# Two pairs of a feed-forward layer as eight block products, and the order of loads and splits at the turn to its down projection

## The chip, the cores and the metric

One core of a Trainium2 chip runs the whole program. The metric is the device time of one execution in microseconds (us). Engines are named PE (TensorE, matrix products), DVE (VectorE), ACT (ScalarE), POOL (GpSimd) and SP (SyncE, which issues the DMAs).

## The reference, cut to what matters

The program is one step of a two-layer decoder over 1024 prompt tokens and 8 x 4 sample tokens, 1056 in all, in float32 with a model width of 1024 and an inner width of 2816. Each layer has a mixer, a feed-forward block with a convolution over three tokens, and a gate. The change lies in the feed-forward block:

```python
def conv_ffn(xn, prefix, w_up, conv_w, conv_b, w_down):
    u = xn @ w_up                                   # (tokens, 5632)
    ext = jnp.concatenate([prefix, u], axis=1)
    c = conv_b + ext[:, 0:L] * conv_w[0]
    for k in range(1, CONV_W):
        c = c + ext[:, k:k + L] * conv_w[k]
    gate, val = jnp.split(c, 2, axis=-1)
    return (jax.nn.gelu(gate) * val) @ w_down, ext[:, -CONV_BUF:]
```

## The kernel before, in words

**Products.** Tokens lie in the free dimension, channels in the partitions, in tiles of 128. A float32 product is made of three products of rounded parts: high x high, low x high and high x low; for that every operand is split, the high part by a copy on ACT, the low part by a subtraction on DVE (`parts_of`, L585 and L586, in the up projection; `split`, L145 and L146, for the down weights).

**The up projection.** `ffn` walks over 22 pairs, each a gate tile and the value tile that belongs to it. A pair is a 2 x 2 block product: the 1024 channels in two halves of four tiles, the tokens in two halves N1 and N2 of 528 (H). `prod` (L666) is one block product over four channel tiles, 4 x 3 parts x 2 chunks of 264 columns = 24 matmuls (L672). `plain`, which pair 0 uses, takes eight such products, 192 matmuls. `unit`, used by pairs 1 to 21, takes seven, 168 matmuls, in the manner of Strassen and Winograd; for that it needs sums of weight blocks (`sums`, L603 to L606, on POOL, new for each pair) and sums of token blocks T1 to T4 (`token_sums`, L618, with DVE lines L640 to L643, splits at L647 and L648; `first_sums`, L655), formed once per layer from the normalized tokens. T1 overwrites the N2 half of the first four channel tiles of `xh` and `xl`, so it can be written only when `plain` has read them; T2 and T3 go into tiles `tk`, T4 into `t4h` and `t4l`. In `token_sums` the raw sums use the scratch of the convolution (`cg`, `ext`, `t4`). Results X, Y, Z and `aux` leave PSUM into `ext` (L699 on DVE in layer 0, L697 on ACT in layer 1), and the convolution runs on them: one step on ACT (L709), two on DVE (L711), for the gate `cg` and the value `cv`, then gelu (L716) and the product (L721), whose result `act_out` stores in DRAM as `ad`. Layer 0 scales by the norm factor R after the products, layer 1 before them (`normed`).

**The turn.** The last unit calls `end()`, which is `turn` (L828): `act_in` loads the activations of inner tiles 0 and 1 back (`ar`) and splits them into `ah` and `al`; `down_block` loads and splits a block of the down weights (`wr` into `wh` and `wl`); the residuals `hd` are loaded back into `h` by eight DMAs. Then `down` (L885) forms `mm` (L162) and adds it to `h` (L907), with 36 matmuls for the first two tiles of `h`.

**Order.** Each engine runs its instructions in program order. That order is made by a scheduler which simulates a timeline and places each instruction where its time comes up; `tc.issue_after` forces one instruction behind another. `late` is a list of instructions behind which the first splits are held.

## Time and profile before

| | us |
|---|---|
| median of 3 runs (2258.25 to 2262.13) | 2260.67 |
| the profiled execution | 2264.66 |
| its span | 2262.8 |
| PE busy in the span | 2170.3 (96%) |
| DVE busy | 1709.6 (76%) |
| ACT busy | 994.3 (44%) |
| POOL busy | 723.1 (32%) |

The profiled execution is 4 us above the median; what lies outside its span is 1.9 us. Times within the span, such as 133.10, are counted from its start. The granted clock of PE is given as a share of 2.4 GHz.

### The profile page before, as it was taken

How to read it: one execution, taken by the hardware profiler on the slowest of the kernel's cores; microseconds unless marked ns; L12 is line 12 of the kernel's file. 1: busy time of each engine (PE TensorE's matmuls, PEld its weight loads, DVE VectorE, ACT ScalarE, POOL GpSimd, SP SyncE). 2: the span in 40 equal slices, each digit the busy share in tenths (PEclk: the TensorE clock that was granted, in tenths of full speed). 3: DMA queues.
4: the chain of work that ended last, by engine and by line, in shares of the span. 5: the costliest groups of instructions: out<-in, count | busy, mean ns of one | idle time of the engine just before them, and what ended most of it. 6: DMA issues, size and time to landing. Idle time of an engine off the chain costs nothing.

```text
span 2262.8 us, 38188 instructions
## 1 busy us (share of the span) xinstructions
PE 2170.3 (96%) x15141; PEld 2112.4 (93%) x15141; DVE 1709.6 (76%) x2435; ACT 994.3 (44%) x1815; POOL 723.1 (32%) x752
## 2 busy tenths in 40 slices
PE   8979999999999999999989998899999999999999
PEld 7879999999899999999977898899999999999898
DVE  5889999999756677567689629788888876666843
ACT  6543343434321235346689625545454542121532
POOL 1435555554000013313467432544443420000400
PEclk7889999999999999999999999899999999999999
DMA  4322222222662311322111342122222227222121
GB/s 143 112 57 67 77 86 77 76 77 77 226 213 86 105 57 62 100 62 42 38 40 36 116 122 72 48 86 72 81 77 86 77 104 217 90 90 82 57 84 40
DMA packets 220006, 198.95 MB, mean 88 GB/s; under 512 B 38899, under 2 KB 190276, under 8 KB 219659
## 3 DMA queue, kind: packets, MB, share of 16 engines
q1 hardware_dynamic: 219827, 196.51, 27.9%
q8 instruction: 119, 1.95, 0.4%
q14 instruction: 60, 0.49, 0.1%
HBM read 150.42 MB, written 51.59 MB: 89 GB/s over the span
## 4 chain that ended last, share of the span: by engine, by line
PE 78%; DVE 14%; ACT 4%; issue 2%; POOL 1%; DMA 1%; SPq 0%; ACTq 0%; DVEq 0%; POOLq 0%
PE mm L162 22%; PE x L672 11%; PE y L672 10%; PE z L672 10%; PE aux L672 5%; PE ub L168 3%; PE ub L170 3%; PE ub L169 3%; DVE xl L225 2%; PE dps L359 2%; PE qkp L168 1%; PE qkp L170 1%; PE qkp L169 1%; DVE h L917 1%; DVE wl L146 1%
## 5 line engine op out<-in xcount | busy, mean ns | idle before, releaser
L907 DVE TENSOR_TENSOR h<-mm,h 128x1056 f32<-128x1056 f32 x160 | 200.6, 1256 | 159.7 <-PE mm L162 159.7
L242 POOL TENSOR_TENSOR acc<-acc,sq 128x352 f32<-128x352 f32 x84 | 92.0, 1099 | 640.0 <-ACT sq L241 638.6
L162 PE MATMUL mm<-ah,wh 128*128 128x352 f32 x960 | 209.8, 328 | 11.8 <-ACT ah L585 10.1
L162 PE MATMUL mm<-al,wh 128*128 128x352 f32 x960 | 208.6, 325 | 0.0
L162 PE MATMUL mm<-ah,wl 128*128 128x352 f32 x960 | 206.8, 324 | 0.0
L711 DVE SCALAR_TENSOR_TENSOR cg<-ext,cw,cg 128x1072 f32<-128x1072 f32 x88 | 181.7, 2065 | 4.7 <-ACT cg L709 4.6
L145 ACT ACTIVATE wh<-wr 128x1024 fp32r<-128x1024 f32 x77 | 81.1, 1055 | 236.2 <-PE mm L162 203.9
L162 PEld LDWEIGHTS mm<-ah,wh 128*128 128x128 f32 x960 | 164.1, 190 | 14.1 <-ACT ah L585 10.5
L692 POOL COPY sto<-ext 128x2 f32<-128x2 f32 x88 | 57.0, 648 | 338.4 <-ACT ext L697 202.7
L162 PEld LDWEIGHTS mm<-al,wh 128*128 128x128 f32 x960 | 164.6, 190 | 0.4 <-DVE al L586 0.4
L162 PEld LDWEIGHTS mm<-ah,wl 128*128 128x128 f32 x960 | 163.7, 189 | 0.0
L672 PE MATMUL x<-xl,wh 128*128 128x264 f32 x704 | 146.2, 289 | 3.6 <-DVE xl L1626 3.6
L672 PE MATMUL x<-xh,wh 128*128 128x264 f32 x704 | 146.2, 290 | 2.7 <-ACT p L749 1.3
L672 PE MATMUL x<-xh,wl 128*128 128x264 f32 x704 | 145.7, 288 | 0.0
L168 PE MATMUL ub<-xh,wh 128*128 128x352 f32 x432 | 142.1, 329 | 0.1
L170 PE MATMUL ub<-xh,wl 128*128 128x352 f32 x432 | 140.5, 325 | 0.0
L169 PE MATMUL ub<-xl,wh 128*128 128x352 f32 x432 | 139.4, 323 | 0.0
L691 POOL COPY ext<-sin 128x16 f32<-128x16 f32 x88 | 81.2, 922 | 139.2 <-DVE cg L711 61.3
L711 DVE SCALAR_TENSOR_TENSOR cv<-ext,cw,cv 128x1072 f32<-128x1072 f32 x88 | 120.6, 1370 | 3.7 <-ACT cv L709 3.1
L585 ACT ACTIVATE ah<-ar 128x1024 fp32r<-128x1024 f32 x88 | 51.8, 636 | 160.6 <-PE mm L162 141.1
L672 PEld LDWEIGHTS x<-xl,wh 128*128 128x128 f32 x704 | 112.0, 192 | 4.2 <-DVE xl L1626 4.1
L672 PEld LDWEIGHTS x<-xh,wh 128*128 128x128 f32 x704 | 111.5, 193 | 3.7 <-ACT p L749 1.6
(391 smaller groups left out, 6578.6 us busy)
## 6 DMA issues: line engine op xcount, KB each, us to landing
ad<-cv SPq DMA_DIRECT2D x44, 536.0 KB
ar<-ad SPq DMA_DIRECT2D x44, 536.0 KB
wr<-in_w_up_dram SPq DMA_DIRECT2D x46, 512.0 KB
wr<-in_w_down_dram SPq DMA_DIRECT2D x44, 512.0 KB
vr<-in_w_up_dram SPq DMA_DIRECT2D x42, 512.0 KB
h<-hd SPq DMA_DIRECT2D x24, 528.0 KB
wr<-in_w_ple_gate_dram SPq DMA_DIRECT2D x16, 512.0 KB
hd<-h SPq DMA_DIRECT2D x13, 528.0 KB
```

Of the source, the lines that this page charges most:

```text
L145: A.activation(out=wh, in_=flat, func=AF.Copy)
L162: PE.matmul(ps[:, c, :C], w[k], b[k][:, c * C:(c + 1) * C], start=st, stop=sp)
L168: PE.matmul(ps, wh[k], bh[k][:, cs], start=k == 0, stop=False)
L169: PE.matmul(ps, wh[k], bl[k][:, cs], start=False, stop=False)
L170: PE.matmul(ps, wl[k], bh[k][:, cs], start=False, stop=k == nk - 1)
L242: G.tensor_tensor(out=st["acc"][:, cs], in0=st["acc"][:, cs], in1=sq, op=ALU.add)
L585: A.activation(out=h_, in_=src, func=AF.Copy)
L672: PE.matmul(ps[c], x[:, k0 + k, :], y[k][:, c * HC:(c + 1) * HC], start=first and n == 0, stop=n == 11, skip_group_check=True)
L691: G.tensor_copy(out=es[:, :, 0:2], in_=sin[:, j, :].rearrange("p (s r) -> p s r", r=2))
L692: G.tensor_copy(out=sto[:, j, 0:2], in_=e[:, NP:NP + 2])
L711: V.scalar_tensor_tensor(out=c, in0=e[:, k:k + CO], scalar=cw[:, k, j:j + 1], in1=c, op0=ALU.mult, op1=ALU.add)
L907: V.tensor_tensor(out=three(hm_(f, m)), in0=ps[:, :, :C], in1=three(hm_(f, m)), op=ALU.add)
```

## The change

Pair 1 becomes a second `plain`, so that units run from pair 2 on, all in one order of products; the special order that unit 1 had (L785 to L799) is gone. `token_sums` is called twice, for channel tiles 0 and 1 within pair 0 and 2 and 3 within pair 1, with scratch of its own, `tt`, which has one buffer; `first_sums` follows pair 1's products. At the turn the first weight block's DMA is issued behind the second activation load, the last gate convolution and the last `act_out` behind the second activation's split on ACT, and the residual loads, as before, behind that load.

```diff
@@ -615,16 +618,12 @@
-        def token_sums():
-
-            t1s = []
-            for k in range(4):
+        def token_sums(ks):
+
+            for k in ks:
                 K = k + 4
-                if k % 2:
-                    t2, t3, t4 = exts[0][:, 2:2 + H], exts[0][:, 2 + H:2 + T], exts[1][:, 2:2 + H]
-                else:
-                    c = long("cg", CO)
-                    t2, t3, t4 = c[:, :H], c[:, H:T], long("t4", H)
+                tt = long("tt", 3 * H)
+                t2, t3, t4 = [tt[:, n * H:(n + 1) * H] for n in range(3)]
...
@@ -727,8 +725,7 @@
-            t1s = token_sums()
-            first_sums(t1s)
+            token_sums(range(2 * i, 2 * i + 2))
             times(two(eg[:, 2:2 + H]), x_ps, two(R1))
@@ -737,6 +734,8 @@
             cg = gate_conv(i)
             times(two(ev[:, 2:2 + H]), z_ps, two(R1))
+            if i:
+                first_sums()
             act_out(i, cg)
@@ -760,46 +759,29 @@
-            if i > 1:
-                prod(Y, wc, 4, T2, True)
...
-            else:
-
-                prod(Z, wb, 4, B22, True)
-                A.activation(out=two(p5), in_=z_ps, func=AF.Copy)
...
-            cg = gate_conv(i)
+            prod(W, wv, 0, T4, True)
+            es = ExitStack()
             if not more:
-                end()
+                es.enter_context(tc.issue_after(end().ins))
+            with es:
+                cg = gate_conv(i)
@@ -807,7 +789,10 @@
             if more:
                 wv_ = val_parts(raws.pop(0))
-            act_out(i, cg)
+                act_out(i, cg)
+            else:
+                with tc.issue_after(pre[1].ins):
+                    act_out(i, cg)
@@ -833,17 +819,17 @@
             act_in(0)
-            came = act_in(1)
-            pre.append(down_block(0, 0))
+            came, split_ = act_in(1)
+            pre.extend([down_block(0, 0, came), split_])
             pairs(f)
             with tc.issue_after(came.ins):
                 for m in range(DT):
                     dma(hm_(f, m), hd[m])
+            return split_
@@ -856,12 +842,15 @@
-        S = sums(w1)
         plain(0, wg, wv)
         late.clear()
-        w = (big_parts(w1[0]), s12_parts(S), big_parts(S[:, 1024:2048]), val_parts(w1))
-        raws = [load(2)]
-        for i in range(1, FT):
+        w2 = load(2)
+        wg, wv = big_parts(w1[0]), big_parts(w1[1])
+        S = sums(w2)
+        plain(1, wg, wv)
+        w = (big_parts(w2[0]), s12_parts(S), big_parts(S[:, 1024:2048]), val_parts(w2))
+        raws = [load(3)]
+        for i in range(2, FT):
             w = unit(i, *w, raws, turn)
@@ -886,7 +875,7 @@
-                return pre.pop() if pre else down_block(g, half)
+                return pre.pop(0) if g + half == 0 else down_block(g, half)
```

Three places of the order. In the rows of the changed kernel line numbers are its own: L670 is L672 of before, L697 is L699, L709 is L711, L707 is L709, L714 is L716, L719 is L721, L588 and L589 are L585 and L586, L804 and L805 are the halves of the activations' split, L860 is L871, L896 is L907, L789 is L807 and L787 is L805.

PE where pair 0 ends in layer 0, before; `vh` and `vl` are the split value weights of pair 1:

```order
L672 MATMUL z<-xh,wh 128x264 x2
L672 MATMUL z<-xl,wh 128x264 x2
L672 MATMUL z<-xh,wl 128x264 x2
L672 MATMUL aux<-t4h,vh 128x264 x2
L672 MATMUL aux<-t4l,vh 128x264 x2
L672 MATMUL aux<-t4h,vl 128x264 x2
```

Z is pair 0's last product; `aux` is the first of pair 1's.

The same place now:

```order
L670 MATMUL z<-xh,wh 128x264 x2
L670 MATMUL z<-xl,wh 128x264 x2
L670 MATMUL z<-xh,wl 128x264 x2
L670 MATMUL x<-xh,wh 128x264 x2
L670 MATMUL x<-xl,wh 128x264 x2
L670 MATMUL x<-xh,wl 128x264 x2
```

What follows pair 0's Z was the product with T4; now it is pair 1's X with the plain tokens.

DVE beside it in layer 0, before: token sums and their splits, in a row:

```order
L641 SCALAR_TENSOR_TENSOR cg<-h,gains,u_1423 128x528
L642 SCALAR_TENSOR_TENSOR cg<-h,gains,cv 128x528
L648 TENSOR_TENSOR t4l<-ext_1152,t4h 128x528
L641 SCALAR_TENSOR_TENSOR ext_1151<-h,gains,vv 128x528
L642 SCALAR_TENSOR_TENSOR ext_1151<-h,gains,cv 128x528
L643 SCALAR_TENSOR_TENSOR t_1422<-h,gains,cg 128x528
L643 SCALAR_TENSOR_TENSOR ext_1152<-h,gains,ext_1151 128x528
```

Nothing but sums and one split of a sum stands in this stretch.

DVE where the changed kernel has reached the sums of the third channel tile:

```order
L647 TENSOR_TENSOR tk<-tt,tk 128x528
L709 SCALAR_TENSOR_TENSOR cg<-ext_1151,cw_80,cg 128x1072
L647 TENSOR_TENSOR t4l<-tt,t4h 128x528
L589 TENSOR_TENSOR wl<-vr,wh 128x1024
L709 SCALAR_TENSOR_TENSOR cv<-ext_1152,cw_80,cv 128x1072
L640 SCALAR_TENSOR_TENSOR tt<-h,gains,p_1402 128x528
L641 SCALAR_TENSOR_TENSOR tt<-h,gains,cv 128x528
L697 TENSOR_TENSOR ext_1151<-x,R 128x528
L709 SCALAR_TENSOR_TENSOR cv<-ext_1152,cw_80,cv 128x1072
L642 SCALAR_TENSOR_TENSOR tt<-h,gains,tt 128x528
L639 TENSOR_TENSOR u_1653<-cv 128x528
L719 TENSOR_TENSOR cv<-cg,cv 128x1072
```

Evictions (`ext`), convolution steps (`cg`, `cv`) and a split of pair 1's weights (`wl`) now stand between the sums.

ACT at the turn of layer 0, before (`p` is a combination of products, `wh` a down weight, `cg` and `cv` the last convolution):

```order
L767 ACTIVATE p_6102<-z 128x528
L145 ACTIVATE wh<-wr 128x1024 x2
L709 ACTIVATE cg<-ext_1151,cw_80 128x1072
L709 ACTIVATE cv<-ext_1152,cw_80 128x1072
L585 ACTIVATE ah<-ar 128x1024
L585 ACTIVATE ah<-ar 128x32
L716 ACTIVATE cg<-cg 128x1072
L585 ACTIVATE ah<-ar 128x1024
L585 ACTIVATE ah<-ar 128x32
```

Both splits of down weights stand ahead of the convolution, the activations' splits behind it.

ACT there now:

```order
L765 ACTIVATE p_6102<-z 128x528
L804 ACTIVATE ah<-ar 128x1024
L588 ACTIVATE ah<-ar 128x32
L804 ACTIVATE ah<-ar 128x1024
L588 ACTIVATE ah<-ar 128x32
L707 ACTIVATE cg<-ext_1151,cw_80 128x1072
L707 ACTIVATE cv<-ext_1152,cw_80 128x1072
L145 ACTIVATE wh<-wr 128x1024
L714 ACTIVATE cg<-cg 128x1072
L804 ACTIVATE ah<-ar 128x1024
```

First come the splits of two activations, then the convolution, then one split of weights.

DVE there, before:

```order
L146 TENSOR_TENSOR wl<-wr,wh 128x1024
L805 TENSOR_TENSOR p_6101<-aux,vv 128x264 x2
L711 SCALAR_TENSOR_TENSOR cg<-ext_1151,cw_80,cg 128x1072
L807 TENSOR_TENSOR ext_1152<-p_6101,R 128x528
L711 SCALAR_TENSOR_TENSOR cg<-ext_1151,cw_80,cg 128x1072
L871 STREAM_TRANSPOSE cv<-sto 128x704
L711 SCALAR_TENSOR_TENSOR cv<-ext_1152,cw_80,cv 128x1072
L586 TENSOR_TENSOR al<-ar,ah 128x1024
L586 TENSOR_TENSOR al<-ar,ah 128x32
L711 SCALAR_TENSOR_TENSOR cv<-ext_1152,cw_80,cv 128x1072
L586 TENSOR_TENSOR al<-ar,ah 128x1024
```

The weights' low part `wl` leads, the low parts `al` stand among convolution steps.

DVE there now:

```order
L787 TENSOR_TENSOR p_6101<-aux,vv 128x264 x2
L789 TENSOR_TENSOR ext_1152<-p_6101,R 128x528
L805 TENSOR_TENSOR al<-ar,ah 128x1024
L589 TENSOR_TENSOR al<-ar,ah 128x32
L860 STREAM_TRANSPOSE cv<-sto 128x704
L805 TENSOR_TENSOR al<-ar,ah 128x1024
L589 TENSOR_TENSOR al<-ar,ah 128x32
L709 SCALAR_TENSOR_TENSOR cg<-ext_1151,cw_80,cg 128x1072
L709 SCALAR_TENSOR_TENSOR cv<-ext_1152,cw_80,cv 128x1072
L709 SCALAR_TENSOR_TENSOR cg<-ext_1151,cw_80,cg 128x1072
L146 TENSOR_TENSOR wl<-wr,wh 128x1024
L709 SCALAR_TENSOR_TENSOR cv<-ext_1152,cw_80,cv 128x1072
```

On both engines the splits of `ah` and `al` moved ahead of the last convolution and the split of the down weights behind most of it.

## Rows read from the trace of the kernel before

**Rows 1.** the page, busy time of each engine, and ACT's weight splits

```profile
PE 2170.3 (96%) x15141; PEld 2112.4 (93%) x15141; DVE 1709.6 (76%) x2435; ACT 994.3 (44%) x1815; POOL 723.1 (32%) x752
...
L145 ACT ACTIVATE wh<-wr 128x1024 fp32r<-128x1024 f32 x77 | 81.1, 1055 | 236.2 <-PE mm L162 203.9
```

**Rows 2.** PE's waits: engine, line, released by; total us, times, longest

```profile
PE aux L672 <- DVE t4l L648: 13.0, 5, 6.4
PE mm L162 <- ACT ah L585: 10.1, 2, 5.1
PE aux L672 <- ACT t4h L647: 8.9, 3, 4.8
```

**Rows 3.** timeline, PE, pair 1: start, length, instruction [idle before, releaser]

```profile
133.62 0.51 PE L672 MATMUL aux<-t4h,vh 128*128 128x264 f32 x2 [0.52 <-ACT t4h L647]
...
144.99 0.81 PE L672 MATMUL aux<-t4l,vh 128*128 128x264 f32 x2 [6.36 <-DVE t4l L648]
...
1411.81 0.93 PE L672 MATMUL aux<-t4h,vh 128*128 128x264 f32 x2 [2.23 <-ACT ext L697]
```

**Rows 4.** timeline, turn of layer 0: PE, ACT, DVE

```profile
589.62 2.13 PE L162 MATMUL mm<-ah,wh 128*128 128x352 f32 x6 [4.91 <-ACT ah L585]
...
598.04 0.75 PE L162 MATMUL mm<-ah,wh 128*128 128x352 f32 x3 [0.70 <-DVE h L907]
...
587.34 1.28 ACT L709 ACTIVATE cv<-ext,cw 128x1072 f32<-128x1072 f32 x1 [2.54 <-DVE ext L807]
...
585.31 1.33 DVE L711 SCALAR_TENSOR_TENSOR cg<-ext,cw,cg 128x1072 f32<-128x1072 f32 x1
...
594.17 1.27 DVE L721 TENSOR_TENSOR cv<-cg,cv 128x1072 f32<-128x1072 f32 x1
```

**Rows 5.** timeline, turn of layer 1: PE, ACT, DVE

```profile
1863.21 2.13 PE L162 MATMUL mm<-ah,wh 128*128 128x352 f32 x6 [5.15 <-ACT ah L585]
...
1872.77 0.77 PE L162 MATMUL mm<-ah,wh 128*128 128x352 f32 x3 [0.71 <-DVE h L907]
...
1862.10 1.18 ACT L585 ACTIVATE ah<-ar 128x1024 fp32r<-128x1024 f32 x2 [1.99 <-DMA ar<-ad]
...
1866.92 1.27 DVE L721 TENSOR_TENSOR cv<-cg,cv 128x1072 f32<-128x1072 f32 x1
```

**Rows 6.** timeline, PE, same row of Z in two neighbouring units, layer 0

```profile
558.16 0.41 PE L672 MATMUL z<-xh,wh 128*128 128x264 f32 x2
...
578.67 0.41 PE L672 MATMUL z<-xh,wh 128*128 128x264 f32 x2
```

**Rows 7.** windows, layer 0: length; PE, PEld, DVE, ACT, POOL busy (count); clock; DMA

```profile
133.10:157.10 24.00, 10.43 (x44) 8.99 (x45) 23.12 (x31) 9.42 (x14) 8.41 (x7) 0.57 0.00 1
183.00:283.00 100.00, 98.43 (x803) 97.95 (x803) 98.01 (x104) 40.25 (x44) 55.38 (x52) 1.00 0.24 76
283.00:383.00 100.00, 100.00 (x821) 100.00 (x820) 98.97 (x105) 40.49 (x45) 53.28 (x50) 1.00 0.25 81
133.10:584.70 451.60, 436.46 (x3528) 434.33 (x3528) 433.27 (x467) 181.74 (x201) 225.77 (x209) 0.98 0.23 75
```

**Rows 8.** windows, layer 1, same columns

```profile
1409.60:1432.70 23.10, 11.67 (x44) 9.98 (x45) 21.05 (x24) 11.00 (x21) 14.91 (x9) 0.56 0.08 23
1457.00:1557.00 100.00, 100.00 (x822) 100.00 (x821) 85.90 (x75) 49.92 (x68) 50.57 (x53) 1.00 0.24 77
```

**Rows 9.** groups of DVE by form, 283 to 483: count, busy us, mean ns

```profile
L586 DVE TENSOR_TENSOR wl<-S,wh 128x1024 fp32r<-128x1024 f32 x10 | 12.2, 1219 | 0.0
...
L759 DVE TENSOR_TENSOR vv<-y,p 128x528 f32<-128x528 f32 x10 | 7.0, 697 | 0.0
```

**Rows 10.** timeline, pair 1 of layer 0: DVE's L641 twice, POOL's weight sum

```profile
127.10 0.76 DVE L641 SCALAR_TENSOR_TENSOR cg<-h,gains,p 128x528 f32<-128x528 f32 x1
...
144.85 1.78 DVE L641 SCALAR_TENSOR_TENSOR ext<-h,gains,vv 128x528 f32<-128x528 f32 x1
...
138.10 2.90 POOL L603 TENSOR_TENSOR S<-vr 128x512 f32<-128x512 f32 x1 [6.23 <-DVE wl L586]
```

More of the change, by code (lines that the diff above doesn't have):

```diff
@@ L147, in split, with block @@
         return wh, wl
-    def block(src, k):
+    def block(src, k, first=None):
         raw = wp.tile([P, 1024], F32, name="wr")
-        dma(raw.rearrange("p (k m) -> p k m", k=k), src)
+        with ExitStack() as es:
+            if first is not None:
+                es.enter_context(tc.issue_after(first.ins))
+            dma(raw.rearrange("p (k m) -> p k m", k=k), src)
         with ExitStack() as es:
@@ L649, in token_sums, with first_sums @@
                 t1s.append(t1)
-            return t1s
-        def first_sums(t1s):
+        def first_sums():
             for k, t in enumerate(t1s):
@@ L655, in first_sums @@
                 V.tensor_tensor(out=xl[:, k, N2], in0=t, in1=xh[:, k, N2].bitcast(F32), op=ALU.subtract)
-        tks = []
+        tks, t1s = [], []
         def operand(n, ks):
@@ new lines, in unit @@
+            prod(Y, wc, 4, T2, True)
+            V.tensor_tensor(out=two(u2), in0=y_ps, in1=two(p1), op=ALU.add)
+            prod(Z, wc, 0, T1, True)
+            A.activation(out=two(p5), in_=z_ps, func=AF.Copy)
+            if more:
+                wc_ = s12_parts(S)
+            prod(X, wa, 4, B21, False)
+            first_gate()
+            if more:
+                wa_ = big_parts(raws[0][0])
+            prod(Y, wb, 0, T3, False)
+            third()
+            prod(Z, wb, 4, B22, False)
@@ L799, in unit @@
+            V.tensor_tensor(out=two(u2), in0=z_ps, in1=two(u2), op=ALU.add)
+            second(i, eg, u2)
+            if more:
                 wb_ = big_parts(S[:, 1024:2048])
-            cg = gate_conv(i)
+            prod(W, wv, 0, T4, True)
+            es = ExitStack()
             if not more:
-                end()
+                es.enter_context(tc.issue_after(end().ins))
+            with es:
+                cg = gate_conv(i)
             to = ev[:, 2:2 + H] if normed else p1
```

39 lines of the change are left out of this document (5 added, 34 removed).

## The prediction

> **What bounds the kernel now.** I read the page's shares first: TensorE (PE) is busy 96% of the span, VectorE (DVE) 76%, so a gain must come from PE's remaining idle or slow time, or from fewer matmuls [rows 1]. Second, PE's waits: the three longest after each other are the product with the token sum T4 waiting for its low part from DVE (13.0 us), `mm` waiting for the split activations at the turn to the down projection (10.1 us) and T4's high part from ScalarE (ACT) (8.9 us) [rows 2]. Third, the timeline says where: all T4 waits lie in pair 1, right behind pair 0, once per layer; pair 0 ends at 133.62 - 0.52 = 133.10 in layer 0 and at 1411.81 - 2.23 = 1409.58 in layer 1 [rows 3]. The up projection ends where the turn's idle time begins: 589.62 - 4.91 = 584.71 and 1863.21 - 5.15 = 1858.06 [rows 4, 5].
>
> What an undisturbed unit costs: the same first row of Z in two neighbouring units stands at 558.16 and 578.67, 20.51 us for 168 matmuls, 0.1221 us each [rows 6]. Between pair 0's end and the turn each layer runs 21 units, 3528 matmuls, which is 430.7 us at that rate. Layer 0 takes 451.60, so 20.9 us are lost [rows 7]; layer 1 takes 1858.06 - 1409.58 = 448.5, so 17.8 us are lost. The windows place it: in 133.1 to 157.1 PE is busy 10.43 us with 44 matmuls at a granted clock of 0.57, while DVE is busy 23.12 of 24; 44 matmuls are worth 5.4 us, so 18.6 of the 20.9 are lost there, a further 1.6 in 183 to 283 (98.43 of 100) [rows 7]. In layer 1 the window of 23.1 us holds 44 matmuls at a clock of 0.56, 17.7 us lost [rows 8]. So the price of pair 1 is both the waits and the slow level (matmuls at the 1.2 GHz level round each wait), and it is DVE that PE waits for: it forms, splits and writes 16 token sums of 528 tokens per layer.
>
> **The change, part 1: pair 1 as eight products.** Pair 1 now needs no token sum, only the operands that pair 0 used. It adds 24 matmuls per layer: 24 x 0.1221 = 2.9 us, on PE's path, nothing hides it. In return 192 matmuls (23.4 us) stand between pair 0 and the first unit that needs sums.
>
> Do the sums fit beside it? In the new order on PE the last rows of T2 and T4 stand about 129 matmuls behind pair 1's end. PE gives DVE 192 + 129 = 321 matmuls, 39.2 us, from 133.1 on. DVE's work in that time, layer 0: the 23.1 us of the old window [rows 7], plus eight convolution steps of pairs 0 and 1 at 1.33 [rows 4], 10.6, less about 1.7 of them that the old window already held, plus two products at 1.27 [rows 4], 2.5, two splits of pair 1's weights at 1.22, 2.4, and pair 1's evictions, about four times 0.70, 2.8 [rows 9]: an estimate of 39.7 us. That is 0.5 us more than PE gives: a once-only slip, between 0 and some 4 us.
>
> Then the rest of layer 0. DVE was busy 433.27 of 451.60 us [rows 7]. A pair as eight products saves it four adds at 0.70 and one and a half weight splits of 1.22 [rows 9], with one more scaling about 5 us; 428.3 remain. PE's bound is 430.7 + 2.9 + 1.6 = 435.2, a gain of 16.4; DVE would then have to be busy 98.4% of it. In the steady windows it is at 98.01 and 98.97% [rows 7]. At 98.0% the stretch takes 437.0, a gain of 14.6. I take 14.5, near DVE's bound, because DVE starts unit 2 with no reserve. Layer 1's DVE is at 85.9% in the steady window [rows 8], its sums are formed without gains, so PE's bound counts there: 17.8 - 2.9 = 14.9; I take 14.4.
>
> Removed with it: one set of four weight sums per layer on POOL (32% busy), worth nothing by itself. The new scratch tile `tt` has one buffer: the sums of k must be split before those of k+1 are formed. The queue behind it is DVE's, where convolutions and evictions of pairs 0 and 1 stand between as fill, so I count nothing; if ACT's half of a split were late, one slot would cost a split's 0.70 us, 16 at most per layer in the whole of the 39.2.
>
> DVE and POOL meet. At 127.10 a sum (L641) takes 0.76 us, at 144.85 the same operation takes 1.78, while POOL forms weight sums (one of them 2.90 us long) [rows 10]. The Trainium skill, page "SBUF — State Buffer", section "Who interferes with whom", states that a VectorE instruction with two inputs in SBUF and a GpSimd instruction that reads SBUF exclude each other, and the loser waits for the whole instruction; these rows agree. That rule speaks against forming sums of tokens beside sums of weights, and what it would do here is rival B.
>
> **Part 2: the turn.** Now the first activations are loaded and split ahead, and the weights' split waits behind the last convolution's two activations on ACT and behind three convolution steps on DVE. Layer 0: the last convolution's activation ends at 587.34 + 1.28 = 588.62 [rows 4] at the latest (DVE's scaling ahead of it moves 1.33 forward, so it may end about 587.5); the split of the weights, 1.06 [rows 1], follows; PE starts near 588.6 instead of 589.62. The low part: from 585.31 to 594.17 DVE ran four convolution steps, L807, a transpose and the splits of `al` [rows 4]; in the new order the same work without one step, and then the weights' 1.22: 594.17 - 1.33 + 1.22 = 594.1. PE has 12 matmuls without the low part; before, six took 2.13 us at the slow level [rows 4], so those 12 are through by 592.9, and PE waits about 1.2 us again. 24 remain; before, PE took up to 598.04 - 0.70 = 597.34 for all 36 [rows 4]. From 594.1 at 0.16 us (the faster level there, an estimate from 36 - 12 matmuls in 597.34 - 593.5) they end at 597.9. The second group needs only its first tile back, free earlier. Layer 0: between -0.5 and +2, taken as 0. Here the wait has only changed its name.
>
> Layer 1: ACT stood idle 1.99 us for the load of `ar` after the convolution ended (1862.10 - 1.99 = 1860.11) [rows 5]. With the loads ahead, the weights' split runs 1860.1 to 1861.2 and PE starts there instead of at 1863.21. DVE's low part comes at 1866.92 - 1.33 + 1.22 = 1866.8 [rows 5]; 12 matmuls end about 1865.4, then 1.4 us of waiting. The 36 took 1872.77 - 0.71 - 1863.21 = 8.85 us before, 0.246 each; 24 more from 1866.8 end between 1870.7 (0.16 each) and 1872.7: a gain of 0 to 2, taken as 1. On SP's queue the loads of residuals, eight of them, now stand ahead of the second block of weights; it is needed some 15 us later, and if it is late the price is a wait of 1 to 3 us per layer.
>
> **Sum.** -14.5 - 14.4 - 1 = -29.9. The profiled execution took 2264.66 (2262.8 of it span) and would come to 2234.8; the median of the runs, 4 us lower, to 2230.8. Forecast 2231.
>
> **Rivals.**
> A, the forecast (chance 72%): 2226 to 2237, by DVE's bound in layer 0 (14.5, up to 16.4 or down to 11) and the turn (-3 to +3).
> B, contention of POOL and DVE (14%): in the new order two sets of weight sums, of pairs 2 and 3, fall into the time of the token sums, where one did. A slowed DVE operation costs 1.02 us more [rows 10]; I take four per set, 4 us, and the second set's 4 to 6 as lost in both layers: 2231 + 8 to 11, about 2240. For it: DVE has no reserve in layer 0. Against it: PE's order pushes the uses of sums behind other products, and layer 1's DVE has 14% idle.
> C, the turn's wait really goes (7%): PE starts as soon as the up projection ends, less some 4 us per layer of the 10.1 [rows 2]: about 2223. Against it: ACT's and DVE's new orders put the weights behind the convolution.
> D, slower (4%): the wait only moves to unit 2. If DVE ends the last sums 17 us or more behind PE's need in layer 0 (15 in layer 1), say because `tt` serializes the sums with their splits, every microsecond saved in pair 1 is lost there, and the extra products stay: +5.9 - 1.0 = +4.9, 2265.6. Against it: my estimate of DVE's work exceeds PE's gift by 0.5 us, not by 17.
> E, no difference to speak of (3%): half of D's lateness with a dearer turn.
>
> **How the numbers follow.** The likeliest is A, 2231. Range: A with B's usual end and C's: 2223 to 2242, leaving out D, E and the tails. Faster by over 0.2% (4.5 us, about what a measurement tells from no change): A, B and C, 0.93; within: 0.03; slower: 0.04.
>
> **What would show it.** Right: in the new trace no wait of PE for `t4h` or `t4l` above 3 us; 192 matmuls of pair 1 in about 23.4 us at full clock; DVE at 98% or more from 133 to 565; the up projection of layer 0 some 14 us and of layer 1 some 14 us shorter; at the turn PE's first wait for `wh` of L145 rather than `ah`, and a second for `wl`. Wrong: a wait of over 5 us on `tk`, `t4l` or on the eviction of Y behind the sums in unit 2 (B or D); a steady unit longer than 20.5 us in layer 0 (DVE became the bound for good, then 2240 and more); waits on a down block's load behind the residuals at the second half of the first weights.

## The result and the profile after

The changed kernel takes 2227.62 us (median of 4 runs, 2227.39 to 2228.1), the kernel before in the same comparison 2261.4 us (4 runs, 2258.25 to 2262.91). The ratio is 0.9853 with a 95% interval of 0.9836 to 0.987: faster, 3.4 us below the forecast of 2231 and inside its range. The profiled execution took 2227.78 us, 2225.8 of it span. As the section on the stages shows, some 5 us of this difference are not the change's.

The page's first line of the changed kernel, busy time of each engine, answers to [rows 1]:

```profile
PE 2162.7 (97%) x15189; PEld 2109.6 (95%) x15189; DVE 1683.6 (76%) x2419; ACT 987.2 (44%) x1810; POOL 713.5 (32%) x744
```

PE is again the bound. It has 48 matmuls more than before and is busy 7.6 us less. In the two up projections it is busy 4.8 us less, because matmuls that ran at the slow clock level now run at the full one; in the start of the program, which the section on the stages takes up, it is busy 4.6 us less (92.04 us for 96.67), and in the other stages 1.9 us more.

PE's waits over the whole span (releaser; total us, times, longest) answer to [rows 2]:

```profile
PE mm L165 <- ACT wh L145: 8.6, 2, 4.3
...
PE mm L165 <- DVE wl L146: 2.2, 3, 1.4
```

No wait on a token sum is left; `t4l` and `t4h`, 21.9 us together before, are gone from the list. At the turn `ah` has gone too, and `wh` and `wl` stand there instead, 10.8 us for 10.1.

The up projection as one window of the kernel before, layer 0 and layer 1 (length; PE, PEld, DVE, ACT, POOL busy with counts; granted clock, DMA share, GB/s):

```profile
107.04:584.71 477.67, 461.50 (x3723) 458.74 (x3722) 456.68 (x499) 195.07 (x220) 240.20 (x226) 0.98 0.25 78
1375.69:1858.06 482.37, 464.77 (x3723) 461.23 (x3722) 403.65 (x389) 242.89 (x342) 200.48 (x216) 0.97 0.23 74
```

The same two stretches of the changed kernel:

```profile
101.97:565.04 463.07, 460.87 (x3747) 459.58 (x3746) 441.56 (x490) 189.80 (x216) 232.23 (x222) 1.00 0.26 81
1355.57:1823.48 467.91, 460.58 (x3747) 458.73 (x3746) 391.82 (x378) 237.97 (x341) 198.60 (x211) 0.99 0.25 81
```

Each layer's gain can be read from two numbers in a row, the length and PE's busy time. In layer 0 PE's idle time falls from 477.67 - 461.50 = 16.2 us to 463.07 - 460.87 = 2.2, which is 14.0 us. PE's busy time falls by 0.63 us although 24 products of 0.122 us, 2.93 us, have come in, so 3.6 us were slow time at the lower clock. 14.0 + 3.6 - 2.9 = 14.6 us. In layer 1 the idle time falls by 17.60 - 7.33 = 10.3, the slow time by 4.2 + 2.9 = 7.1, and 10.3 + 7.1 - 2.9 = 14.5.

Windows of layer 0 of the changed kernel, same columns: pair 1, the first unit behind it, a steady stretch, and all from the end of pair 0 to the turn. They answer to [rows 7]; the first and the last begin 0.11 us behind pair 0's end, which is at 127.99:

```profile
128.10:151.60 23.50, 23.50 (x195) 23.50 (x194) 23.42 (x34) 13.24 (x17) 6.80 (x6) 1.00 0.22 69
151.60:172.00 20.40, 20.40 (x170) 20.40 (x169) 19.77 (x20) 10.76 (x15) 8.76 (x6) 1.00 0.16 53
272.00:372.00 100.00, 100.00 (x821) 100.00 (x820) 98.96 (x105) 40.37 (x45) 53.51 (x49) 1.00 0.25 81
128.10:565.04 436.94, 434.74 (x3553) 433.67 (x3551) 420.34 (x458) 179.51 (x202) 217.37 (x202) 1.00 0.24 79
```

In pair 1 PE is busy in all of its 23.50 us at clock 1.00, where before 24 us held 44 matmuls at 0.57. The steady window reads as before.

### The stages of all runs

Every kernel's profiled execution is cut at the same places. "Start" ends with pair 0's first product in layer 0; "up" runs from there to the moment when PE falls idle at the turn; "idle" is PE's first wait there; "rest 0" reaches to the next mixer of layer 1, "mid" to pair 0 of layer 1, "tail" from the first down product of layer 1 to the end. All in us, each edge read from PE's timeline.

| kernel | start | up 0 | idle 0 | rest 0 | mid | up 1 | idle 1 | tail | span |
|---|---|---|---|---|---|---|---|---|---|
| before | 107.04 | 477.67 | 4.91 | 240.40 | 545.67 | 482.37 | 5.15 | 399.59 | 2262.8 |
| changed | 101.97 | 463.07 | 4.31 | 241.23 | 544.99 | 467.91 | 4.31 | 398.01 | 2225.8 |
| changed, second time (`e8_again`) | 108.85 | 462.90 | 4.31 | 243.62 | 545.03 | 467.91 | 4.31 | 394.57 | 2231.5 |
| pairs only (`e1_pairs`) | 103.23 | 462.85 | 4.92 | 239.61 | 545.00 | 467.94 | 5.07 | 401.18 | 2229.8 |
| turn only (`e2_turn`) | 107.04 | 477.83 | 4.31 | 242.02 | 543.89 | 482.82 | 4.31 | 399.38 | 2261.6 |
| weights ahead (`e3_w_ahead`) | 103.29 | 463.01 | 1.97 | 245.18 | 545.04 | 467.94 | 1.97 | 399.80 | 2228.2 |
| three plain pairs (`e4_three`) | 102.04 | 462.65 | 4.31 | 244.24 | 545.69 | 469.61 | 4.31 | 396.05 | 2228.9 |
| more POOL work (`e5_pool`) | 103.03 | 469.52 | 4.31 | 242.32 | 545.76 | 476.60 | 4.31 | 397.95 | 2243.8 |
| convolution late, free (`e6_conv_late`) | 103.14 | 462.89 | 6.59 | 246.85 | 543.43 | 467.60 | 6.03 | 401.77 | 2238.3 |
| convolution late, held (`e7_conv_late`) | 107.06 | 463.01 | 1.97 | 247.54 | 543.37 | 467.62 | 1.97 | 402.06 | 2234.6 |
| convolution and states late (`e9_state_late`) | 101.81 | 463.10 | 1.97 | 245.86 | 543.56 | 467.88 | 1.97 | 403.35 | 2229.5 |

The up projections are the steadiest columns: wherever pair 1 is a plain pair and nothing else is done to them, they repeat within 0.4 us. The start is the least steady: 101.8 to 108.9 us in code that is the same in all these kernels up to pair 1 as far as PE's order goes, and 101.97 and 108.85 in two profiles of one and the same kernel. So of the 37.0 us between the spans of before and after, 29.06 are the up projections', 5.07 the start's, and the rest is spread over the turns, "mid" and the tail.

### The profile page after: what moved, and what is told of

It is laid out like the page before. It is cut to its first block, busy times and chain, and to the rows that moved or that the text cites. A ratio compares the mean times of both kernels' runs of the same rounds, so it can differ in the third digit from the quotient of the medians.

```text
span 2225.8 us, 38235 instructions
## 1 busy us (share of the span) xinstructions
PE 2162.7 (97%) x15189; PEld 2109.6 (95%) x15189; DVE 1683.6 (76%) x2419; ACT 987.2 (44%) x1810; POOL 713.5 (32%) x744
## 4 chain that ended last, share of the span: by engine, by line
PE 81%; DVE 11%; ACT 3%; issue 2%; POOL 1%; DMA 1%; SPq 0%; ACTq 0%; DVEq 0%; POOLq 0%
PE mm L165 23%; PE y L670 11%; PE z L670 10%; PE x L670 10%; PE aux L670 6%; PE ub L171 3%; PE ub L172 3%; PE ub L173 3%; DVE xl L228 2%; PE dps L362 2%; PE qkp L171 1%; PE qkp L172 1%; PE qkp L173 1%; DVE h L906 1%; DVE cg L709 1%
## 5 line engine op out<-in xcount | busy, mean ns | idle before, releaser
L896 DVE TENSOR_TENSOR h<-mm,h 128x1056 f32<-128x1056 f32 x160 | 200.8, 1255 | 154.4 <-PE mm L165 154.4
L709 DVE SCALAR_TENSOR_TENSOR cg<-ext,cw,cg 128x1072 f32<-128x1072 f32 x88 | 180.0, 2046 | 0.0
L670 PE MATMUL x<-xl,wh 128*128 128x264 f32 x704 | 144.9, 287 | 3.4 <-DVE xl L1615 3.4
L670 PE MATMUL x<-xh,wh 128*128 128x264 f32 x704 | 144.6, 287 | 0.6 <-ACT xh L1614 0.6
L670 PE MATMUL x<-xh,wl 128*128 128x264 f32 x704 | 144.4, 287 | 0.0
L689 POOL COPY ext<-sin 128x16 f32<-128x16 f32 x88 | 87.1, 991 | 137.5 <-DVE cg L709 54.9
L709 DVE SCALAR_TENSOR_TENSOR cv<-ext,cw,cv 128x1072 f32<-128x1072 f32 x88 | 123.0, 1397 | 4.2 <-ACT cv L707 3.4
L804 ACT ACTIVATE ah<-ar 128x1024 fp32r<-128x1024 f32 x44 | 46.6, 1060 | 168.7 <-PE mm L165 152.1
L670 PEld LDWEIGHTS x<-xl,wh 128*128 128x128 f32 x704 | 110.6, 190 | 4.2 <-DVE xl L1615 4.1
L670 PEld LDWEIGHTS x<-xh,wh 128*128 128x128 f32 x704 | 110.6, 191 | 0.8 <-ACT xh L1614 0.8
```

The lines of the kernel that those rows point to most:

```text
L670: PE.matmul(ps[c], x[:, k0 + k, :], y[k][:, c * HC:(c + 1) * HC], start=first and n == 0, stop=n == 11, skip_group_check=True)
L689: G.tensor_copy(out=es[:, :, 0:2], in_=sin[:, j, :].rearrange("p (s r) -> p s r", r=2))
L709: V.scalar_tensor_tensor(out=c, in0=e[:, k:k + CO], scalar=cw[:, k, j:j + 1], in1=c, op0=ALU.mult, op1=ALU.add)
L804: split_ = A.activation(out=ah[:, :NP], in_=r[:, :NP], func=AF.Copy)
L896: V.tensor_tensor(out=three(hm_(f, m)), in0=ps[:, :, :C], in1=three(hm_(f, m)), op=ALU.add)
```

## The experiments

### The changed kernel again: how far one comparison reaches (`e8_again`)

No edit.

> The changed kernel once more, beside the others on one chip. The stretch ahead of pair 0 of layer 0 is the same code in all kernels and took 107.04 us in the profile before and 101.97 in that of the changed kernel. Theory (that difference is none of the change's): it falls anywhere from 102 to 107 again, and the time anywhere from 2227 to 2233. Rival (the change moves it): 102 again, 2227 to 2228.5.

Measured: 2233.4 us median (4 runs, 2228.61 to 2233.51) against 2260.64; ratio 0.9871 (0.9855 to 0.9888). The time lies just above the expected range and the start, 108.85 us, 1.9 us above it, so the rival, that the change shortened the start, falls. The profile's start is 6.88 us longer than in the first profile of this kernel, "rest 0" 2.39 longer and its tail 3.44 shorter, all in the same code. The windows around PE's small first products show what differs in the start, this profile first, then the changed kernel's first profile, with 66 and 65 matmuls of the same sequence (columns as above):

```profile
25.00:43.00 18.00, 16.45 (x66) 13.86 (x66) 9.01 (x25) 12.02 (x30) 2.37 (x1) 0.50 0.38 122
```

```profile
25.00:39.50 14.50, 12.93 (x65) 10.83 (x63) 8.26 (x23) 11.18 (x30) 2.38 (x1) 0.67 0.49 153
```

Almost the same matmuls took 18.0 us at a granted clock of 0.50, the 1.2 GHz level throughout, and 14.5 us at 0.67; the kernel before has 65 matmuls at 0.50 in the same 18.0 us. So medians of one kernel taken in different comparisons can stand 6 us apart, and a difference of 2 or 3 us between two variants is not to be read from their medians, only from a stage that repeats. The two results for the changed kernel, 33.8 and 27.2 us below, lie on either side of the forecast gain of 29.9.

### The pairs alone (`e1_pairs`)

The changed kernel with the turn of before:

```diff
-            es = ExitStack()
+            cg = gate_conv(i)
             if not more:
-                es.enter_context(tc.issue_after(end().ins))
-            with es:
-                cg = gate_conv(i)
+                end()
...
-                act_out(i, cg)
-            else:
-                with tc.issue_after(pre[1].ins):
-                    act_out(i, cg)
+            act_out(i, cg)
...
-            came, split_ = act_in(1)
-            pre.extend([down_block(0, 0, came), split_])
+            came = act_in(1)
+            pre.append(down_block(0, 0))
```

> Only the first part: pair 1 as eight products and the split token sums; the turn is that of the kernel before. Theory (the pairs carry the gain, the turn next to none of it): 28 to 31 us below the kernel before; in the profile the two up projections 14 to 15 us shorter each from pair 0's start, PE's wait at each turn 4.9 to 5.2 us for ah again. Rival (the turn's new order is worth several us, by a higher clock in the down projection behind it): only 24 to 27 us below.

Measured: 2234.75 (2231.69 to 2237.0) against 2260.82, ratio 0.9891 (0.9876 to 0.9906), 26.1 below. By the median that is 2 us short of my expectation's lower end. By the stages it is exact: both up projections stand at the changed kernel's length (462.85 and 467.94) and the waits at the turn are those of before (4.92 and 5.07 for 4.91 and 5.15). This edit carries the gain; the missing 2 us are within what start and tail vary by.

### The turn alone (`e2_turn`)

Before, with the changed order of loads and splits at the turn (the last hunks of the diff ahead of the prediction, from `es = ExitStack()` on, and nothing of `plain`, `token_sums` and `unit`).

> Only the second part: pair 1 with seven products as before, the turn with activations first. Theory: within 3 us of the kernel before, 0 to 1 us in layer 0 and 1 to 2.4 us in layer 1 faster. Rival (the turn is worth more): 4 to 7 us faster. The forecast's other side: the one weight block preloaded instead of more comes late, 1 to 3 us slower per layer.

Measured: 2262.31 (11 runs, 2258.3 to 2265.84) against 2260.82, ratio 1.0009 (1.0 to 1.0017): no gain. PE's waits of this kernel in its first down projection (584 to 830):

```profile
PE mm L165 <- ACT wh L145: 4.3, 1, 4.3
PE mm L165 <- DVE wl L146: 2.0, 1, 2.0
```

The first wait is 0.6 us shorter than before (4.3 for 4.91) and a second of 2.0 has come up behind it. Idle time and rest of layer 0 together are 246.33 us for 245.31, of layer 1 and the tail 403.69 for 404.74: +1.0 and -1.1.

### Can the turn's wait go by splitting the weights ahead of the convolution? (`e3_w_ahead`)

The whole last convolution is held behind both halves of the weights' split instead of the activation's:

```diff
-                es.enter_context(tc.issue_after(end().ins))
+                end()
+                for ins in both:
+                    es.enter_context(tc.issue_after(ins.ins))
...
-                with tc.issue_after(pre[1].ins):
+                with tc.issue_after(both[0].ins), tc.issue_after(both[1].ins):
                     act_out(i, cg)
...
-            pre.extend([down_block(0, 0, came), split_])
+            pre.append(down_block(0, 0, came))
+            both[:] = lastsplit
```

> The changed kernel, with the last gate convolution and the last product held behind the split of the first down weights on both engines, where the change holds them behind the activations' split on ScalarE. Theory (the turn's wait only changed its name because the weights' split stands behind the convolution): PE's first wait at each turn falls from 4.31 to about 2 us, its second wait (wl) to under 1, the whole is 5 to 8 us faster than the changed kernel, 2220 to 2223. Rival (another wait stands right behind, the activations' low part or the residuals' load): within 2 us of the changed kernel.

Measured: 2231.13 (2225.7 to 2233.79) against 2260.82, ratio 0.9869 (0.9853 to 0.9884), no faster than the changed kernel. PE's timeline of this kernel at the turn of layer 0 (start, length, instruction, [idle before, releaser]):

```profile
568.27 1.25 PE L165 MATMUL mm<-ah,wh 128*128 128x352 f32 x3 [1.97 <-ACT wh L145]
...
572.19 0.75 PE L165 MATMUL mm<-ah,wl 128*128 128x352 f32 x3 [0.18 <-DVE wl L146]
...
578.34 1.10 PE L165 MATMUL mm<-ah,wh 128*128 128x352 f32 x3 [2.00 <-DVE h L898]
```

DVE's timeline of this kernel beside it:

```profile
572.05 1.32 DVE L709 SCALAR_TENSOR_TENSOR cg<-ext,cw,cg 128x1072 f32<-128x1072 f32 x1
...
575.79 1.33 DVE L709 SCALAR_TENSOR_TENSOR cv<-ext,cw,cv 128x1072 f32<-128x1072 f32 x1
577.03 1.25 DVE L898 TENSOR_TENSOR h<-mm,h 128x1056 f32<-128x1056 f32 x1
```

The wait on `wh` did fall, from 4.31 to 1.97 us, and the one on `wl` to 0.18. But a third grew: 2.00 us on `h`, that is on the addition that takes a finished `mm` out of PSUM (0.70 before [rows 4], none listed for the changed kernel). Four steps of the convolution, 572.05 to 577.03, now stand ahead of the first such addition on DVE. The first 36 products have filled the two `mm` tiles in PSUM that the kernel has, and PE stands until one is taken out. In layer 1 the same wait is 1.99 us. "Idle 0" and "rest 0" together are 247.15 us, 1.6 more than in the changed kernel's first profile (245.54) and 0.8 less than in its second (247.93): no gain. The rival held, though the wait behind is another than the two that I had named. The convolution has moved from in front of the products to in front of their removal.

### The convolution behind the first down group (`e6_conv_late`, `e7_conv_late`, `e9_state_late`)

If DVE's work is what counts, the last pair's convolution might be put where DVE has time. In `e6_conv_late`, which goes out from `e3_w_ahead`, the last pair's convolution stands behind the second group of activation loads in the code, so that the scheduler places it; the first down products do not need it. The buffers of later use are opened behind it:

```diff
             if not more:
                 end()
-                for ins in both:
-                    es.enter_context(tc.issue_after(ins.ins))
-            with es:
+            else:
                 cg = gate_conv(i)
...
+            if g == 1:
+                act_out(FT - 1, gate_conv(FT - 1))
```

> The changed kernel with the whole last convolution and product written behind the first group of the down projection (buffers of later use opened behind it). Theory (the turn is bounded by VectorE's work ahead of the first additions to the residual, of which the four convolution steps are 5.3 us): the first 36 matmuls end 3 to 6 us sooner after the up projection's end than in the changed kernel, 2219 to 2224 in all. Rival (the second weight block or the residuals come too late then): PE waits for wl or for h behind the first 36 matmuls, within 2 us of the changed kernel.

Measured: 2244.11 (2240.29 to 2248.85) against 2260.64, ratio 0.9925 (0.9911 to 0.9939), slower than the changed kernel. PE's waits of this kernel over the whole span:

```profile
PE mm L165 <- ACT wh L145: 12.6, 2, 6.6
PE mm L165 <- DVE wl L146: 9.6, 2, 4.8
```

With nothing to hold it the scheduler still placed the gate's half of the convolution ahead of the weights' split, on DVE (two steps from 567.31 on) and on ACT (its gelu at 570.52, `wh` at 571.52), and the waits became longer, the rival's wait on `wl` among them. `e7_conv_late` is `e6_conv_late` with the convolution held by a forced order behind both halves of the weights' split:

```diff
             if g == 1:
-                act_out(FT - 1, gate_conv(FT - 1))
+                with tc.issue_after(both[0].ins), tc.issue_after(both[1].ins):
+                    act_out(FT - 1, gate_conv(FT - 1))
```

> As the run with the convolution behind the first down group, but also held behind the first weights' split on both engines. Theory: PE's wait at the turn about 2 us, the low part of the weights ready some 4 us sooner than in the changed kernel, 36 matmuls end 4 to 6 us sooner per layer, 2218 to 2223. Rival: as for that run, the second weight block or the additions to h come late instead, within 2 us of the changed kernel.

Measured: 2237.94 (2236.34 to 2241.0) against 2260.64, ratio 0.99 (0.9886 to 0.9914). PE's timeline of this kernel in layer 0, and the DMA issues on SP's queue beside it (start, length, DMA):

```profile
572.04 1.23 PE L165 MATMUL mm<-ah,wh 128*128 128x352 f32 x3 [1.97 <-ACT wh L145]
...
590.17 1.25 PE L165 MATMUL mm<-ah,wh 128*128 128x352 f32 x3 [4.41 <-ACT wh L145]
...
570.01 10.61 SPq L101 DMA_DIRECT2D out_dram<-cv  x16
580.72 1.50 SPq L101 DMA_DIRECT2D ar<-ad  x2
```

No gain: the first wait is 1.97 us, but from 585.76 on PE waits 4.41 us for the weights of the second half, as the rival had it. SP stands for 10.61 us on sixteen writes of the convolution's state (`out_dram<-cv`), and the loads of the next activations and weights (`ar`, `wr`) begin only behind them, at 580.72. `e9_state_late`, which goes out from that, holds the state writes and the convolution behind the eighth addition of the first down group:

```diff
+                        adds.append(V.tensor_tensor(...))
...
             if g == 1:
-                with tc.issue_after(both[0].ins), tc.issue_after(both[1].ins):
+                with tc.issue_after(both[0].ins), tc.issue_after(adds[7].ins):
                     act_out(FT - 1, gate_conv(FT - 1))
+                with tc.issue_after(adds[7].ins):
+                    for n in range(2):
+                        ...
```

> The changed kernel with the last convolution, the last product and the writing of the convolution states behind the first eight additions to the residual on VectorE, and the state's sixteen small DMAs so behind the loads of the second group. Theory (VectorE's steps ahead of the first additions bound the turn, and with the state writes out of SP's way nothing takes their place): PE's first wait 2 us per turn, the low part's under 0.5, no wait over 2 us in the first 72 matmuls; 4 to 8 us faster than the changed kernel in its two runs (2227.6 and 2233.4). Rival (a wait of the second half's weights or of h takes its place): within 2 us of it.

Measured: 2233.22 (2231.61 to 2235.99) against 2259.14, ratio 0.9888 (0.9872 to 0.9905): no gain over the changed kernel, as the rival had it. Windows of the first 12 and 60 us from the turn of layer 0, this kernel first, then the changed kernel (columns as above):

```profile
564.91:576.91 12.00, 10.04 (x53) 10.04 (x54) 7.53 (x10) 7.18 (x9) 0.00 (x0) 0.86 1.01 396
564.91:624.91 60.00, 53.15 (x315) 51.63 (x316) 45.24 (x51) 19.56 (x29) 0.00 (x0) 0.97 0.60 196
```

```profile
565.04:577.04 12.00, 6.28 (x27) 5.82 (x28) 11.86 (x14) 7.37 (x9) 0.00 (x0) 0.72 0.93 322
565.04:625.04 60.00, 53.58 (x322) 52.21 (x323) 45.28 (x51) 20.85 (x34) 0.00 (x0) 0.94 0.70 216
```

In the first 12 us the start is really better: 53 matmuls for 27, at a clock of 0.86 for 0.72. The lead does not last. Of the 315 and 322 matmuls in 60 us, 9 and 18 belong to another step (`aux<-ident,pt`), which leaves 306 and 304 products of the down projection. Counted on PE's timeline from the turn, the 73rd of these begins at 15.19 us for 19.37, the 289th at 56.92 for 57.37, the 433rd at 84.31 for 83.50. In between PE waits 2.79 us on `h`, up to 602.49, behind the convolution. DVE is busy 45.2 us of the 60 in both. So moving one late operation did not lower the turn's cost: each place that was tried handed PE a wait of 2 to 5 us elsewhere in the first groups of the down projection. That the convolution's steps on DVE have to be paid somewhere there is my reading of `e3_w_ahead` and this run; in `e7_conv_late` the late part was SP's queue.

### A third plain pair (`e4_three`)

If DVE's backlog still costs in the changed kernel, one more pair without token sums must cost less than its 24 products, 2.9 us, per layer:

```diff
         wg, wv = big_parts(w1[0]), big_parts(w1[1])
-        S = sums(w2)
         plain(1, wg, wv)
-        w = (big_parts(w2[0]), s12_parts(S), big_parts(S[:, 1024:2048]), val_parts(w2))
-        raws = [load(3)]
-        for i in range(2, FT):
+        w3 = load(3)
+        wg, wv = big_parts(w2[0]), big_parts(w2[1])
+        S = sums(w3)
+        plain(2, wg, wv)
+        w = (big_parts(w3[0]), s12_parts(S), big_parts(S[:, 1024:2048]), val_parts(w3))
+        raws = [load(4)]
+        for i in range(3, FT):
```

`first_sums` follows pair 2 there.

> The changed kernel with a third pair as eight products, so that the token sums have two pairs of time. It adds 24 matmuls of 0.122 us per layer, 5.9 us in all. Theory (the sums were in time already but for the 2.1 us of PE's waits in unit 2 and 3 of layer 0): 3 to 6 us slower than the changed kernel. Rival (VectorE's backlog costs more than the waits behind unit 2 show): as fast as the changed kernel or faster.

Measured: 2232.73 (2230.67 to 2233.66) against 2260.82, ratio 0.9878 (0.9864 to 0.9891), the same as the changed kernel within what the comparisons tell. The up projection of layer 0, this kernel (columns as above; the changed kernel's row stands further up):

```profile
102.04:564.69 462.65, 462.65 (x3771) 462.22 (x3770) 439.15 (x484) 188.02 (x212) 233.72 (x218) 1.00 0.26 80
```

24 products more, and yet 0.42 us shorter: 462.65 us with PE busy in all of it. With the third plain pair PE waits for nothing in layer 0, so there the rival holds. What DVE's backlog still cost the changed kernel there is thus 2.93 + 0.42 = 3.4 us, of which 2.2 are idle time. In layer 1 there was nothing to buy: the length grows by 1.7 us, the stretch behind pair 0 by the full 3.0, and pair 0 itself came out 1.3 us shorter. Together the up projections are 1.3 us longer, less than the 3 to 6 of my expectation.

### More work on POOL beside the token sums (`e5_pool`)

Eight additions of weights that nobody reads are added on POOL per layer, written behind the second half of the token sums:

```diff
             token_sums(range(2 * i, 2 * i + 2))
+            if i:
+                for _ in range(8):
+                    G.tensor_tensor(out=junk, in0=w2[1][:, A1], in1=w2[1][:, A2], op=ALU.add)
```

> The changed kernel with eight more additions on GpSimd per layer, each reading two halves of pair 2's weights and writing a tile that nobody reads, placed beside pair 1. Theory (rival B of the prediction: a sum of tokens on VectorE that meets a weight addition on GpSimd takes about 1 us more, and layer 0's VectorE has no reserve before unit 2): the last token sums of layer 0 end 5 to 8 us later and PE waits for them about as long, layer 1 loses 0 to 4; 5 to 11 us slower than the changed kernel. Rival (the order leaves room): under 2 us slower in both layers.

Measured: 2245.58 (2244.01 to 2246.99) against 2260.64, ratio 0.9931 (0.9919 to 0.9943), some 12 to 18 us slower than the changed kernel, going by its two medians, more than I had expected. Both up projections grew, by 6.5 us in layer 0, as expected, and by 8.7 in layer 1, over twice the most that I had expected there. The window from 125 to 175 of layer 0, this kernel first, then the changed kernel:

```profile
125.00:175.00 50.00, 44.97 (x350) 43.82 (x349) 50.00 (x56) 25.68 (x32) 34.68 (x26) 0.97 0.15 44
```

```profile
125.00:175.00 50.00, 50.00 (x411) 50.00 (x410) 48.43 (x62) 27.04 (x35) 17.97 (x18) 1.00 0.17 54
```

POOL works 16.7 us more, DVE has no free moment left, and PE falls from 50.00 to 44.97. The last low part of a sum ends at 175.45, 46.5 us behind pair 0's end for 41.9 in the changed kernel, and PE waits 4.9 us in unit 2. DVE and POOL of this kernel in that stretch show how:

```profile
134.91 1.79 DVE L642 SCALAR_TENSOR_TENSOR tt<-h,gains,cv 128x528 f32<-128x528 f32 x1
...
174.76 0.69 DVE L648 TENSOR_TENSOR t4l<-tt,t4h 128x528 fp32r<-128x528 f32 x1
...
133.13 6.96 POOL L732 TENSOR_TENSOR junk<-vr 128x512 f32<-128x512 f32 x4
```

The sum that takes 0.76 us alone [rows 10] takes 1.79 beside a run of POOL additions. The Trainium skill, page "SBUF — State Buffer", section "Who interferes with whom", states that a VectorE instruction with two inputs in SBUF and a GpSimd instruction that reads SBUF exclude each other; the trace agrees, at a bit over twice the time.

In layer 1 the scheduler placed the additions earlier, beside pair 0, where DVE still forms the low parts of the normalized tokens. DVE and then PE in this kernel, then DVE in the changed kernel:

```profile
1387.56 1.58 DVE L1619 TENSOR_TENSOR xl<-h,xh 128x352 fp32r<-128x352 f32 x1
...
1389.19 0.81 PE L671 MATMUL y<-xl,wh 128*128 128x264 f32 x2 [3.85 <-DVE xl L1619]
```

```profile
1383.22 0.51 DVE L1615 TENSOR_TENSOR xl<-h,xh 128x352 fp32r<-128x352 f32 x1
```

Each of those low parts took 1.58 us for 0.51, and PE waited 3.85, 0.86 and 0.63 us for them, 5.3 together against 2.5 before this edit. All of the 8.7 us lie in pair 0 (42.81 us for 34.12): 3.0 are idle time, the rest is slow time, at a granted clock of 0.76 for 0.90. My expectation for layer 1 was wrong: I had counted on DVE's idle time there, but the idle time lies later, in the steady units, and not beside pair 0.

## Why the prediction was right, and where not

**The bound and the price of pair 1: right.** I took 18.6 us and 17.7 us for what pair 1 lost, partly as waits and partly as slow clock. The up projections fell by 14.60 and 14.46 us against 14.5 and 14.4, and by the same amounts without the new turn (`e1_pairs`: 14.82 and 14.43). The steady unit is 20.50 us as before. These rows of the changed kernel's PE show it, and the end of pair 0 in layer 0 at 127.99:

```profile
127.99 0.40 PE L670 MATMUL x<-xh,wh 128*128 128x264 f32 x2
...
538.49 0.41 PE L670 MATMUL z<-xh,wh 128*128 128x264 f32 x2
...
558.99 0.41 PE L670 MATMUL z<-xh,wh 128*128 128x264 f32 x2
```

**Layer 1's bound: right.** From pair 0's end to the turn the changed kernel takes 433.79 us in layer 1, with PE busy in all of it:

```profile
1389.69:1823.48 433.79, 433.79 (x3554) 433.57 (x3552) 358.67 (x325) 222.08 (x311) 190.62 (x205) 1.00 0.25 81
```

PE's bound was 430.7 + 2.9 = 433.6. The gain there is 14.7 us; pair 0 ahead of it came out 0.2 longer.

**Layer 0's bound: right in size, by luck, and wrong in its reason.** I gave 437.0 us from pair 0's end to the turn, as DVE's bound with 428.3 us of work at 98%. It took 437.05, of which the window above has 436.94. But DVE was busy 420.34 of these, 96.2%, not 98%, so one of my own signs failed. The mis-sized term is DVE's saving: estimated at 5 us, it was 433.27 - 420.34 = 12.9. Grouped by kind of instruction (the lengths of single instructions overlap a little and add up to 11.6), 8.1 us are instructions that fell away, net of those that came in: I had left out the evictions and part of the sums and splits of a unit, and two splits of down weights, 2.4 us, that now come behind the turn. 3.5 us are instructions that became shorter. Two of the groups in layer 0 (count, busy us, mean ns), before:

```profile
L807 DVE TENSOR_TENSOR ext<-p,R 128x528 f32<-128x528 f32 x20 | 32.6, 1629 | 0.0
L586 DVE TENSOR_TENSOR vl<-vr,vh 128x512 fp32r<-128x512 f32 x20 | 31.9, 1595 | 0.0
```

And in the changed kernel:

```profile
L789 DVE TENSOR_TENSOR ext<-p,R 128x528 f32<-128x528 f32 x19 | 28.6, 1505 | 0.0
L589 DVE TENSOR_TENSOR vl<-vr,vh 128x512 fp32r<-128x512 f32 x19 | 28.3, 1489 | 0.0
```

One instruction less in each, which saves 1.6 us each and not the 0.6 or 0.7 of an undisturbed one, and the others are 0.11 to 0.12 us shorter. The raw token sums fell most, from a mean of 1.13 to 0.75 us; others lengthened, the splits of T2 and T3 from 0.70 to 0.97, which goes with POOL's work now meeting other instructions. That the length still came out as forecast has another cause. PE's own bound was 435.2, with 1.6 us of waits taken over from before; the waits that remained were 1.3 us on `u` and 0.8 on `p`, 2.1 us, and another 1.2 us are PE busy longer than its matmuls take at the steady rate. The two bounds stood 1.8 us apart, too close for the length to tell which was in force; DVE's share speaks for PE's, with waits at single instructions. The third plain pair confirms it from the other side: without those waits layer 0's up projection is PE alone. So the step that failed is DVE's busy time as the bound; waits and slow time of 3.3 us where I had 1.6 happened to bring the length to the same place.

**The sums fit beside pair 1: right, by a hair.** I estimated 39.7 us of DVE's work against 39.2 of PE's. In layer 0 the last low part of a sum ended at 169.88, 41.9 us behind pair 0's end, and PE needed it about a microsecond later, at 170.90. Both terms came out larger than I had estimated: PE's order put 351 products ahead of that need, 42.9 us, and not 321. Had it been 39.2, PE would have waited 2.7 us for DVE's 41.9, within the slip of 0 to 4 that I had allowed. DVE's part goes with rival B's mechanism, seen once. Rows of the changed kernel, DVE and then POOL:

```profile
154.28 3.53 DVE L647 TENSOR_TENSOR tk<-tt,tk 128x528 fp32r<-128x528 f32 x2
157.74 1.79 DVE L647 TENSOR_TENSOR t4l<-tt,t4h 128x528 fp32r<-128x528 f32 x1
...
169.18 0.70 DVE L647 TENSOR_TENSOR t4l<-tt,t4h 128x528 fp32r<-128x528 f32 x1
...
153.82 1.69 POOL L606 TENSOR_TENSOR S<-vr 128x512 f32<-128x512 f32 x1 [1.97 <-DVE wl L589]
```

At 154.28 two splits take 3.53 us, and one 1.79, while POOL forms one set of weight sums; at 169.18 the same split takes 0.70. With the convolution step behind them (2.35 us for 1.33) that cost DVE some 4 us, what I had priced for one set; without it the work would have been some 2 us under my estimate. The cost was there, and PE did not feel it because its order puts the uses of the sums behind other products. In layer 1 no wait stands behind pair 0. So both halves of my argument against B held. `e5_pool` shows what B would have been with more POOL work: the same lengthening, no reserve, and then PE waits. B was a live rival, turned down for the right reason, but the margin was about 1 us.

**The turn: right that the wait only changes its name.** PE's rows at both turns of the changed kernel answer to [rows 4, 5]:

```profile
569.35 1.25 PE L165 MATMUL mm<-ah,wh 128*128 128x352 f32 x3 [4.31 <-ACT wh L145]
...
574.65 0.74 PE L165 MATMUL mm<-ah,wl 128*128 128x352 f32 x3 [1.42 <-DVE wl L146]
...
1827.79 1.25 PE L165 MATMUL mm<-ah,wh 128*128 128x352 f32 x3 [4.31 <-ACT wh L145]
...
1832.36 1.25 PE L165 MATMUL mm<-ah,wl 128*128 128x352 f32 x3 [0.68 <-DVE wl L146]
```

First `wh`, then `wl`, as forecast. The second wait is 1.42 and 0.68 for 1.2 and 1.4. The first is 4.31 in both layers, where I expected about 3.9 in layer 0 and 3.1 in layer 1; so layer 1's start came 0.84 us earlier, not 2. The 1 us that I had counted for it stays open, but the table of stages says more than one comparison. "Idle 0" and "rest 0" together are 244.53 and 245.31 us in the two profiles with the old order (`e1_pairs`, before) and 245.54 to 248.55 in the five with the new one (changed twice, `e2_turn`, `e4_three`, `e5_pool`). "Idle 1" and the tail together are 404.74 and 406.25 with the old order and 398.88 to 403.69 with the new. In these profiles the new order is thus some 2 us longer in layer 0, where I had put 0, and some 4 shorter in layer 1, where I had put 1. With two profiles of the old order and a spread of 3 to 5 us within the new one that is an indication, not a result. The edit alone (`e2_turn`) gained nothing, with an upper end of the interval 0.17% to the slower side. Rival C, that the wait really goes, fell: `e3_w_ahead` halved the wait and lost it again to DVE's additions.

**Rivals D and E: fell.** No wait moved to the first unit behind the plain pairs; PE is busy 20.40 of 20.40 us there.

**The number.** The sum gave -29.9. The up projections gave -29.1 for -28.9. The median is 33.8 below; in the profile 5 of 37 us are the start's, which no step of the prediction speaks of; a second comparison gave 27.2. The two medians lie 3.4 us below and 2.4 above the forecast, and where a comparison falls between them is luck. Of the 0.2 us in the stages layer 1's part is earned; layer 0's is the luck told above.

**Open.** What sets the level that the clock is granted in the start and behind the turn, and whether the new turn is worth 1 us, 2 or nothing. Both lie below what these comparisons can tell.

## What to carry to other kernels

Where a cheaper algorithm needs operands that a second engine must first form, using the dear form once more can be worth it: 24 extra products cost 2.9 us, the waits and the slow clock behind them had cost 17.5. Before moving one late operation ahead of another, ask what the moved one will stand in front of: at the turn each order of splits, convolution and additions that was tried gave PE waits that add up to about the same or more. And compare stages that repeat within tenths, not medians from different comparisons, when a few microseconds are at stake.
